# Other staging offsets for a second layer's token tiles, and a loop on three engines issued in source order

## The chip, the cores and the metric

The kernel runs on one core of a Trainium2 chip. TensorE does matmuls and transposes into PSUM (eight banks of 128 x 512 float32), ScalarE, VectorE and GpSimd do the elementwise work, SyncE issues most DMAs. The metric is the device time of one execution in microseconds, median over runs; lower is better.

## The reference

Two layers over 1024 latent tokens and 256 context tokens, width 1024, in float32:

```python
# layer 0: windowed attention, 16 query heads on 4 key heads, a sink logit per head
# layer 1: multi-head latent attention
hx = rms_norm(x, norm_g[i]) * (1.0 + scale_x[:, None]) + shift_x[:, None]
hc = rms_norm(ctx, norm_g[i]) * (1.0 + scale_c) + shift_c
# layer 1, inside project(h):
cq, ckv, kr, g = jnp.split(h @ w_in, [512, 512 + 256, 512 + 256 + 32], axis=-1)
q  = (rms_norm(cq, q_norm) @ w_uq).reshape(b, n, 16, 96)
kv = (rms_norm(ckv, kv_norm) @ w_ukv).reshape(b, n, 16, 128)
# softmax over all 1280 keys, then
yx = (ox * jax.nn.silu(gx)) @ w_out
x = x + gate_x[:, None] * yx
return rms_norm(x, final_g)
```

The change lies where layer 0 ends and layer 1 begins: the tokens that layer 0 has written are read again, normalized, scaled and shifted into `hx`/`hc`, and multiplied with the 288 columns of `w_in` that give the latent keys `ckv` and the rope keys `kr`.

## The kernel before

**Precision.** A float32 operand is kept as two reduced-precision parts, hi and lo. `split` makes them: ScalarE casts hi (L121), another engine subtracts it from the source for lo (L122; VectorE, or GpSimd where the caller says so). A product takes three matmuls (`mm3`, L126 to L128).

**Memory.** There is one hand-laid arena for hi/lo parts (`arena_r`) and one for float32 tiles (`arena_f`, 52 KB per partition). A `Ring` hands out fixed slots of an arena in turn. Stages of the kernel reuse the same bytes, so a tile that is laid over a tile of the stage before waits for the last reader there. Layer 0's attention probabilities are a ring of eight blocks of 2.5 KB, from 14 KB to 34 KB of `arena_f`: block i from 14 + 2.5 i. Each attention unit (a tile of 128 tokens and a key head) takes four blocks in turn; unit 38 takes blocks 0 to 3, the last one, unit 39, blocks 4 to 7. L611 transposes them and is their last reader.

**Layer 1's token tiles.** Ten tiles of 128 tokens go through these steps; two tiles make a pair `p`.
- `norm_x(i)`: load of 512 KB into a slot of ring `xr` (L210), square with sum on ScalarE (L212), a multiply-add on VectorE (L213), the power on GpSimd (L214), the scaling on VectorE (L215).
- `turn_x`: eight transposes on TensorE (L222) in two halves of four; each half takes the next bank of `pst` (6, 7, 6, 7 and so on) and ScalarE copies it (L223) into `xt`, a slot of ring `xtr`.
- `build_h(p)`: for each of eight 128-row blocks a scale-and-shift on VectorE (L236), and after every second one a cast for hi on ScalarE (L239) and a subtraction for lo on VectorE (L241), into `hT1[p]`.
- `kv_tile(ti)`: 24 matmuls of 288 columns from `hT1[p]` and the weights `wt1[0]` into a bank of `pss` (0 to 5); the square on ScalarE (L953), L954 on VectorE, the power on GpSimd (L955), the scaling on VectorE (L992), and the rope keys (L995, or L268 and L273). Its `rest` is put on a list: two transposes (L1005) into the next bank of `pst`, and their `split` (L121 and L122, both reading that bank) into `ckvT`.
- `flush(2)` runs the oldest `rest` while more than two are on the list, so `rest` of tile ti runs in iteration ti + 2.
- `g_tile(6, p)`: 48 matmuls of 256 columns and a silu (L1091), stored to DRAM (L1093).

`fetch1(k)` loads a weight block in pieces through the ring `stg` (L262) and splits each piece. Block 0 is that of `kv_tile`, block 6 that of `g_tile(6, .)`, blocks 1 and 2 those of `cq_tile`, which follows the loop. `wt1[0]`, `hT1[0]` and `hT1[1]` lie over `arena_r` tiles that layer 0's last attention units read; `wt1[6]`, `wt1[1]` and `hT1[2]` to `hT1[4]` lie over the output weights and operands of layer 0's last output projection (L669, L670), which is traced between `build_h(1)` and the loop.

**What orders the work.** The Tile framework tracks which bytes and which PSUM banks each instruction reads and writes and draws the waits. The order of an engine's instructions is chosen by a planner that walks a model of the engines and takes, of what is ready there, what stands first in the source. Inside a region `tc.manual_schedule(engines=...)` the named engines issue the region's instructions in source order; where those of outside fall between them stays with the planner. The second attention, later on, already stands in such a region. The loop around the change does not. Each engine executes its instructions in order: one that waits holds those behind it.

`pst` counts its calls: `turn_x` of tiles 0 to 5 takes 6 and 7 each, `rest` of tile 0 takes 6, `turn_x` of tile 6 takes 7 and then 6, `rest` 1 takes 7, tile 7 takes 6 and 7, `rest` 2 takes 6, tile 8 takes 7 and then 6, `rest` 3 takes 7, tile 9 takes 6 and 7, `rest` 4 takes 6, `rest` 5 takes 7.

Of the kernel before, what the change touches and what calls it, by code (L numbers as in the profile page):

```python
# [22 lines left out]
NT = TOK // 128  # L23
# [24 lines left out]
def shp(ap, *dims):  # L48
    n = 1
    for d in dims:  # L50
        n *= d
    ap = ap[:, 0:n]
    if len(dims) == 1:
        return ap
    names = "abcdefg"[: len(dims)]
    kw = {c: d for c, d in zip(names[1:], dims[1:])}
    return ap.rearrange("p (" + " ".join(names) + ") -> p " + " ".join(names), **kw)
# [3 lines left out]
def kernel(ctx: ExitStack, tc: tile.TileContext, t, out, dbg=None):  # L61
    nc = tc.nc
# [6 lines left out]
    F = cpool.tile([128, F_KB * KB], F32, name="arena_f")  # L69
# [16 lines left out]
    def r_at(kb, *dims):  # L86
        n = int(np.prod(dims))
        return shp(R[:, int(kb * KB) : int(kb * KB) + n], *dims)

    def f_at(kb, *dims):  # L90
        n = int(np.prod(dims))
        return shp(F[:, int(kb * KB) : int(kb * KB) + n], *dims)
# [26 lines left out]
    def split(hi, lo, src, lo_eng=None):  # L119

        nc.scalar.copy(hi, src)  # L121
        (lo_eng or nc.vector).tensor_sub(lo, src, hi.bitcast(F32))  # L122

    def mm3(o, a, b, first, last):
        (ah, al), (bh, bl) = a, b
        nc.tensor.matmul(o, ah, bh, start=first, stop=False)  # L126
        nc.tensor.matmul(o, al, bh, start=False, stop=False)  # L127
        nc.tensor.matmul(o, ah, bl, start=False, stop=last)  # L128
# [79 lines left out]
    def norm_x(src, xr, junk):  # L208
        x = xr.next()
        load(out=x, in_=src)  # L210
        st = sm_ring()
        nc.scalar.activation(junk, x, AF.Square, accum_out=st[:, 0:1])  # L212
        nc.vector.tensor_scalar(st[:, 1:2], st[:, 0:1], 1.0 / D, EPS, ALU.mult, ALU.add)  # L213
        nc.gpsimd.tensor_tensor(st[:, 2:3], st[:, 1:2], mhalf, ALU.pow)  # L214
        nc.vector.tensor_scalar_mul(x, x, st[:, 2:3])  # L215
        return x

    def turn_x(x, xt, j):
        for q in range(2):
            ps = shp(pst(), 4, 128)  # L220
            for c in range(4):
                nc.tensor.transpose(ps[:, c, :], x[:, (4 * q + c) * 128 : (4 * q + c + 1) * 128], ident)  # L222
            nc.scalar.copy(xt[:, 4 * q : 4 * q + 4, j * 128 : j * 128 + 128], ps)  # L223
# [33 lines left out]
    def load_w(dst, src, stage, nk, n, lo_eng=None, col0=0, k0=0):  # L257

        per = max(1, 512 // n)
        for k in range(k0, nk, per):  # L260
            st = shp(stage.next(), per, n)
            load(out=st, in_=src[k * 128 : (k + per) * 128, col0 : col0 + n].rearrange("(k p) n -> p k n", p=128))  # L262
            split(dst[:, 0, k : k + per, :], dst[:, 1, k : k + per, :], st, lo_eng or nc.gpsimd)

    def rope(o, u, cos, sin, nh, dim, tmp):

        hf = dim // 4
        nc.vector.tensor_mul(o, u, cos.unsqueeze(1).to_broadcast([128, nh, dim]))  # L268
        uv = u.rearrange("p h (a b c) -> p h a b c", a=2, b=2)
        sv = sin.rearrange("p (a b c) -> p a b c", a=2, b=2)  # L270
        tv = tmp.rearrange("p h (a b c) -> p h a b c", a=2, b=2)
        for b in range(2):
            nc.vector.tensor_mul(  # L273
                tv[:, :, :, b, :],
                uv[:, :, :, 1 - b, :],
                sv[:, :, b, :].unsqueeze(1).to_broadcast([128, nh, 2, hf]),
            )
        nc.gpsimd.tensor_add(o, o, tmp)
# [9 lines left out]
    stg = Ring(F, [4, 6, 8], 512)  # L288
    xr = Ring(F, [34, 38, 42, 48], 1024)
    ev = Ring(F, [38, 40, 42, 44], 512)  # L290
    junk = f_at(30, 512).bitcast(BF16)
# [3 lines left out]
    qst = Ring(F, [34, 48], 1024)  # L295
# [10 lines left out]
    class Pieces:  # L306
# [6 lines left out]
        def load(self, n=1):  # L313
            for _ in range(n):
                if self.todo:
                    bi, k = self.todo.pop(0)
                    c0 = blocks[bi]
                    st = shp(stg.next(), 2, 256)
                    src = w_in[k * 128 : (k + 2) * 128, c0 : c0 + 256]
                    load(out=st, in_=src.rearrange("(k p) n -> p k n", p=128))  # L320
                    self.held.append((bi, k, st))
# [370 lines left out]
    E = mybir.EngineType  # L692
# [233 lines left out]
    qn = f_at(8, 512)  # L926
    kvn = f_at(10, 256)
    junk = f_at(34.5, 512).bitcast(BF16)
    stg = Ring(F, [30, 32.25, 49.5], 576)
    xr = Ring(F, [22, 26, 45], 1024)  # L930
    xtr = Ring(F, [14, 37], 2048)
    ev = Ring(F, [2, 4, 6, 12], 512)
    ukK = r_at(134, 2, 2, 1024)
    ukV = r_at(64, 2, 2, 1024)
# [1 line left out]
    def src1(i):  # L936
        return x1_d[i * 128 : i * 128 + 128, :]
# [8 lines left out]
    def fetch1(bi, eng=None):  # L946
        kind, c0, n = blocks1[bi]
        nk = 4 if kind[0] == "q" else 8
        wt1[bi] = r_at(wst1[bi], 2, nk, n)
        load_w(wt1[bi], t["b_w_uq"] if kind[0] == "q" else w_in1, stg, nk, n, lo_eng=eng, col0=c0)  # L950

    def rstd(ps, n, st):
        nc.scalar.activation(junk[:, 0:n], ps, AF.Square, accum_out=st[:, 0:1])  # L953
        nc.vector.tensor_scalar(st[:, 1:2], st[:, 0:1], 1.0 / n, EPS, ALU.mult, ALU.add)  # L954
        nc.gpsimd.tensor_tensor(st[:, 2:3], st[:, 1:2], mhalf, ALU.pow)  # L955
        return st[:, 2:3]
# [18 lines left out]
    def flush(n=0):  # L975
        while len(pend) > n:
            pend.pop(0)()

    def kv_tile(ti):
        p, j = ti // 2, ti % 2  # L980
        W = wt1[0]
        ps = pss()
        for k in range(8):
            mm3(
                ps[:, 0:288],
                [hT1[p][:, s, k, j * 128 : j * 128 + 128] for s in range(2)],
                [W[:, s, k, :] for s in range(2)],
                k == 0, k == 7,
            )
        r = rstd(ps[:, 0:256], 256, sm_ring())  # L990
        e = ev.next()
        nc.vector.scalar_tensor_tensor(e[:, 0:256], ps[:, 0:256], r, kvn, ALU.mult, ALU.mult)  # L992
        kr = krF[:, ti : ti + 1, :]
        if ti < 2:
            nc.vector.tensor_copy(kr, shp(ps[:, 256:288], 1, 32))  # L995
        else:
            rope(
                kr, shp(ps[:, 256:288], 1, 32), cosb[:, ti - 2, :], sinb[:, ti - 2, :], 1, 32,
                shp(e[:, 288:320], 1, 32),
            )  # L1000

        def rest():
            pt = pst()
            for c in range(2):
                nc.tensor.transpose(pt[:, c * 128 : c * 128 + 128], e[:, c * 128 : c * 128 + 128], ident)  # L1005
            ts = slice(ti * 128, ti * 128 + 128)
            split(ckvT[:, 0, :, ts], ckvT[:, 1, :, ts], shp(pt[:, 0:256], 2, 128))

        pend.append(rest)
# [64 lines left out]
    def g_tile(bi, p, half=None, bank=None):  # L1074
        c0 = blocks1[bi][1]
        W = wt1[bi]
        if half != 1:
            gps[bi] = pss() if bank is None else bank
        ps = gps[bi]
        for j in (0, 1) if half is None else (half,):  # L1080
            for k in range(8):
                mm3(
                    ps[:, j * 256 : j * 256 + 256],
                    [W[:, s, k, j * 128 : j * 128 + 128] for s in range(2)],
                    [hT1[p][:, s, k, :] for s in range(2)],
                    k == 0, k == 7,
                )
        if half == 0:
            return
        gg = ev.next()  # L1090
        nc.scalar.activation(gg, ps, AF.Silu)  # L1091
        ch = (c0 - 800) // 128
        load(out=g1_d[ch : ch + 2, :, (p - 1) * 256 : p * 256].rearrange("c p n -> p c n"), in_=shp(gg, 2, 256))  # L1093

    nx = norm_x(src1(4), xr, junk)
    for ti in range(NT):
        n = ti + 3
        if 4 <= n < NT:
            if n % 2 == 0:
                xt = shp(xtr.next(), 8, 256)  # L1100
            turn_x(nx, xt, n % 2)
            if n + 1 < NT:
                nx = norm_x(src1(n + 1), xr, junk)
            if n % 2:
                build_h(n // 2, xt, hT1[n // 2], ada1.A, ada1.B, fast=True)
        kv_tile(ti)
        flush(2)
        if ti > 1 and ti % 2:
            g_tile(6, ti // 2)
    fetch1(2, nc.vector)  # L1110
    for ti in range(8):
        cq_tile(ti)
        flush(2)
    fetch1(3, nc.vector)
    fetch1(4)
    rtmp = Ring(F, [14, 28], 512)
    qst = Ring(F, [16, 20, 24, 37, 41, 45], 1024)
    for ti in range(8):
        qr_tile(ti)
        flush(2)  # L1120
# [368 lines left out]
    E = mybir.EngineType  # L1489
# [174 lines left out]
```

## Time and profile before

| | |
|---|---|
| median of 3 runs | 1632.33 us (1632.14 to 1632.37) |
| the profiled execution | 1635.02 us, of which the profile's span is 1633.2 us |
| TensorE busy over the span | 1587.7 us (97%) |
| VectorE, ScalarE, GpSimd busy | 927.3, 805.0 and 702.5 us |
| mean granted TensorE clock | 0.993 |

The profile is of one execution. Its times count from the start of the span. Of a matmul the engine's start is recorded and its end modelled, so matmuls overlap in the listing; the distance from one start to the next is its pace. A merged row gives the start of the first instruction, the time from there to the end of the last, and their number. A bracket at the end of a row is the engine's idle time just before it and what ended that. Layer 0's attention ends near 724 us, the loop of the change runs from there to about 814 us.

### The profile page before, as it was taken

The page shows a single profiled execution, that of the slowest core. Times are in us where ns is not written, and L with a number is a line of the kernel's source. Part 1 is how long each engine was busy: PE and PEld are TensorE (multiplying, and loading weights), DVE is VectorE, ACT ScalarE, POOL GpSimd, SP SyncE. Part 2 cuts the span into 40 slices and gives each one's busy share as a digit, 9 for nine tenths or more (in the row PEclk, how much of TensorE's full clock was granted, in tenths as well). Part 3 has the DMA queues.
Part 4 walks back from the last instruction along what each step waited for, and adds up shares of the span by engine and source line. Part 5 has one row for each costly group of instructions (what it writes and reads, how often), then busy time and mean ns, then how long its engine had stood idle before and what let it go on. Part 6 is the DMA issues. An engine that isn't in the chain of part 4 may idle for free.

```text
span 1633.2 us, 27119 instructions
## 1 busy us (share of the span) xinstructions
PE 1587.7 (97%) x9938; PEld 1240.4 (76%) x9938; DVE 927.3 (57%) x1993; ACT 805.0 (49%) x1558; POOL 702.5 (43%) x684
## 2 busy tenths in 40 slices
PE   7999999999999999998999999999999999999998
PEld 4787787887878888877998899566766766766587
DVE  3515550538888888868425203566566566566354
ACT  3432232359777777777313323454555554544321
POOL 1241121115453333334105230478687688688510
PEclk9999999999999999999999999999999999999999
DMA  7447774444343333335105743213233223244151
GB/s 247 162 149 214 223 213 144 128 152 107 94 121 94 91 91 91 91 119 188 45 2 167 264 144 91 65 37 94 66 94 83 80 74 94 65 126 116 54 174 65
DMA packets 147205, 192.70 MB, mean 118 GB/s; under 512 B 13936, under 2 KB 84208, under 8 KB 147072
## 3 DMA queue, kind: packets, MB, share of 16 engines
q1 hardware_dynamic: 145456, 188.94, 38.5%
q10 hardware_dynamic: 1616, 2.04, 0.4%
q8 instruction: 78, 1.28, 0.3%
q14 instruction: 55, 0.45, 0.1%
HBM read 144.77 MB, written 46.15 MB: 117 GB/s over the span
## 4 chain that ended last, share of the span: by engine, by line
PE 85%; ACT 5%; DVE 4%; issue 2%; DMA 2%; POOL 1%; ACTq 0%; POOLq 0%; SPq 0%; DVEq 0%
PE PB L126 15%; PE PB L127 14%; PE PB L128 14%; PE PB L1291 11%; PE PB L1313 8%; PE PB L1260 5%; PE PB L621 4%; PE PB L611 3%; PE PB L583 2%; PE PB L584 2%; PE PB L181 2%; ACT arena_f L593 1%; PE PB L1263 1%; ACT arena_r L121 1%; ACT arena_f L632 1%
## 5 line engine op out<-in xcount | busy, mean ns | idle before, releaser
L126 PE MATMUL PB<-arena_r 128*128 128x512 f32 (+3 forms) x1496 | 509.9, 342 | 4.5 <-ACT arena_r L387 1.6
L127 PE MATMUL PB<-arena_r 128*128 128x512 f32 (+3 forms) x1496 | 503.3, 337 | 3.1 <-DVE arena_r L388 1.4
L128 PE MATMUL PB<-arena_r 128*128 128x512 f32 (+3 forms) x1496 | 501.2, 335 | 0.2 <-DVE arena_r L122 0.2
L1305 POOL TENSOR_TENSOR arena_f<-arena_f 128x512 f32<-128x512 f32 x252 | 328.9, 1305 | 110.5 <-ACT arena_f L1297 94.3
L126 PEld LDWEIGHTS PB<-arena_r 128*128 128x128 f32 x1496 | 284.2, 191 | 50.2 <-issue 15.0
L127 PEld LDWEIGHTS PB<-arena_r 128*128 128x128 f32 x1496 | 285.2, 191 | 31.6 <-DVE arena_r L388 3.1
L128 PEld LDWEIGHTS PB<-arena_r 128*128 128x128 f32 x1496 | 285.1, 191 | 28.4 <-DVE arena_r L122 0.4
L1265 DVE TENSOR_REDUCE arena_f<-PB 128x1 f32<-128x1280 f32 x128 | 190.2, 1486 | 118.5 <-PE PB L1263 109.7
L122 POOL TENSOR_TENSOR arena_r<-arena_f,arena_r 128x512 fp32r<-128x512 f32 x88 | 115.5, 1327 | 308.5 <-ACT arena_r L121 250.9
L1291 PE MATMUL PB<-arena_r 64*128 64x512 f32 (+1 forms) x1600 | 230.8, 393 | 2.9 <-ACT arena_f L1297 1.5
L1297 ACT ACTIVATE arena_f<-PB 128x1024 f32<-128x1024 f32 x160 | 164.2, 1027 | 125.5 <-PE PB L1291 85.3
L1291 PEld LDWEIGHTS PB<-arena_r 64*128 64x128 f32 (+1 forms) x1600 | 175.2, 185 | 28.5 <-ACT arena_f L1297 3.3
L590 DVE CUSTOM_DVE_ANT_0 arena_f<-PB,arena_f,small 128x256 f32<-128x256 f32 (+1 forms) x288 | 145.1, 522 | 25.1 <-PE PB L584 18.6
L1313 PE MATMUL PB<-arena_f 128*64 128x512 f32 x640 | 144.4, 597 | 0.0
L122 DVE TENSOR_TENSOR arena_r<-PB,arena_r 128x512 fp32r<-128x512 f32 (+1 forms) x186 | 123.1, 670 | 22.7 <-ACT arena_r L121 22.0
L593 ACT ACTIVATE arena_f<-arena_f,small 128x640 f32<-128x640 f32 (+2 forms) x160 | 119.3, 746 | 28.4 <-DVE small L592 27.5
L621 PE MATMUL PB<-arena_r 128*128 128x512 f32 x336 | 123.6, 440 | 3.5 <-ACT arena_f L632 3.3
L121 ACT CAST arena_r<-arena_f 128x512 fp32r<-128x512 f32 (+2 forms) x137 | 82.2, 609 | 81.1 <-DVE arena_f L485 11.5
L121 ACT CAST arena_r<-PB 128x512 fp32r<-128x512 f32 (+1 forms) x186 | 104.0, 570 | 31.6 <-PE PB L611 30.9
L611 PE MATMUL PB<-ident,arena_f 128*128 128x128 f32 x672 | 111.5, 274 | 1.4 <-ACT arena_f L593 0.9
L1313 PEld LDWEIGHTS PB<-arena_f 128*64 128x64 f32 x640 | 43.1, 136 | 81.3 <-issue 80.5
L611 PEld LDWEIGHTS PB<-ident,arena_f 128*128 128x128 f32 x672 | 83.5, 140 | 20.5 <-ACT arena_f L593 5.1
(180 smaller groups left out, 2002.4 us busy)
## 6 DMA issues: line engine op xcount, KB each, us to landing
arena_f<-ada_w SPq DMA_DIRECT2D x47, 512.0 KB, 5.4
arena_r<-q_d SPq DMA_DIRECT2D x80, 256.0 KB, 4.1
arena_r<-qn_d SPq DMA_DIRECT2D x64, 256.0 KB, 3.7
arena_r<-qr_d SPq DMA_DIRECT2D x192, 64.0 KB, 3.2
arena_f<-a_w_in SPq DMA_DIRECT2D x40, 256.0 KB, 3.4
arena_f<-x SPq DMA_DIRECT2D x16, 512.0 KB, 5.1
g_d<-arena_f SPq DMA_DIRECT2D x32, 256.0 KB, 2.1
q_d<-arena_f SPq DMA_DIRECT2D x64, 128.0 KB, 2.4
```

The lines of the kernel that those rows point to most:

```text
L121: nc.scalar.copy(hi, src)
L122: (lo_eng or nc.vector).tensor_sub(lo, src, hi.bitcast(F32))
L126: nc.tensor.matmul(o, ah, bh, start=first, stop=False)
L127: nc.tensor.matmul(o, al, bh, start=False, stop=False)
L128: nc.tensor.matmul(o, ah, bl, start=False, stop=last)
L611: nc.tensor.transpose(pt[:, h, :], self.Ps[h][:, ci * 128 : ci * 128 + 128], ident)
L621: nc.tensor.matmul(self.pv, V[:, self.chunks[ci], self.g, :], PT[:, s], start=ci == 0 and s == 0, stop=ci == self.m - 1 and s == 1,)
L1265: nc.vector.reduce_max(self.mx[:, 32 + b : 33 + b], flat, AX.X, negate=True)
L1291: nc.tensor.matmul(S[:, t], k[r, c : c + 128], q[r], start=j == 0, stop=j == 4)
L1297: nc.scalar.activation(E, self.S, AF.Exp)
L1305: eng.tensor_add(self.acc, self.acc, E[:, t])
L1313: nc.tensor.matmul(self.pv[p : p + 64], Vq[:, cs[t], self.h % 4, :], E[:, t], start=i == 0, stop=i == 4)
```

## The change

It does three things.
1. The offsets of `stg`, `xr` and `xtr` in `arena_f` are others, and with them those of `rtmp` and `qst` further on, with the same number and size of slots. In KB: `xr` goes from 22, 26, 45 to 48, 14, 18; `xtr` from 14, 37 to 24.25, 38.75; `stg` from 30, 32.25, 49.5 to 36.5, 22, 32.25. 48 to 52 held a gate of layer 0 that only its context tiles use; 38 to 48 hold small tiles of the last attention units.
2. The loop over the ten tiles stands in a region in which TensorE, ScalarE and VectorE issue in source order.
3. In the source `build_h` stands behind `kv_tile` and ahead of `flush`, where it stood ahead of `kv_tile`; and `fetch1(2)`, which followed the loop, stands in its last iteration ahead of the last `g_tile`.

```diff
-    stg = Ring(F, [30, 32.25, 49.5], 576)
-    xr = Ring(F, [22, 26, 45], 1024)
-    xtr = Ring(F, [14, 37], 2048)
+    stg = Ring(F, [36.5, 22, 32.25], 576)
+    xr = Ring(F, [48, 14, 18], 1024)
+    xtr = Ring(F, [24.25, 38.75], 2048)
...
     nx = norm_x(src1(4), xr, junk)
-    for ti in range(NT):
-        n = ti + 3
-        if 4 <= n < NT:
-            if n % 2 == 0:
-                xt = shp(xtr.next(), 8, 256)
-            turn_x(nx, xt, n % 2)
-            if n + 1 < NT:
-                nx = norm_x(src1(n + 1), xr, junk)
-            if n % 2:
+    with tc.manual_schedule(engines={E.PE, E.Activation, E.DVE}):
+        for ti in range(NT):
+            n = ti + 3
+            if 4 <= n < NT:
+                if n % 2 == 0:
+                    xt = shp(xtr.next(), 8, 256)
+                turn_x(nx, xt, n % 2)
+                if n + 1 < NT:
+                    nx = norm_x(src1(n + 1), xr, junk)
+            kv_tile(ti)
+            if 4 <= n < NT and n % 2:
                 build_h(n // 2, xt, hT1[n // 2], ada1.A, ada1.B, fast=True)
-        kv_tile(ti)
-        flush(2)
-        if ti > 1 and ti % 2:
-            g_tile(6, ti // 2)
-    fetch1(2, nc.vector)
+            flush(2)
+            if ti == NT - 1:
+                fetch1(2, nc.vector)
+            if ti > 1 and ti % 2:
+                g_tile(6, ti // 2)
...
-    rtmp = Ring(F, [14, 28], 512)
-    qst = Ring(F, [16, 20, 24, 37, 41, 45], 1024)
+    rtmp = Ring(F, [14, 20], 512)
+    qst = Ring(F, [16, 24.25, 28.25, 39, 43, 47], 1024)
```

## The prediction

> **What bounds the kernel now.** I read the page's busy shares first, then the busy time in stretches around the change, then the timelines of TensorE, ScalarE and VectorE there, and last SyncE's waits.
>
> ```profile
> span 1633.2 us, 27119 instructions
> PE 1587.7 (97%) x9938; PEld 1240.4 (76%) x9938; DVE 927.3 (57%) x1993; ACT 805.0 (49%) x1558; POOL 702.5 (43%) x684
> PE 85%; ACT 5%; DVE 4%; issue 2%; DMA 2%; POOL 1%; ACTq 0%; POOLq 0%; SPq 0%; DVEq 0%
> ...
> 710.00:724.00 14.00, 13.08 (x70) 10.19 (x69) 8.49 (x25) 7.63 (x19) 7.21 (x10) 1.00 0.17 58
> 724.00:739.00 15.00, 13.89 (x70) 10.87 (x69) 10.21 (x28) 12.23 (x27) 3.08 (x4) 1.00 0.89 296
> 739.00:755.00 16.00, 12.38 (x92) 11.42 (x91) 15.15 (x27) 10.84 (x23) 8.57 (x7) 1.00 0.64 203
> 755.00:774.00 19.00, 15.77 (x106) 15.22 (x105) 14.69 (x37) 14.10 (x30) 9.85 (x14) 0.82 0.52 156
> 774.00:800.00 26.00, 26.00 (x211) 26.00 (x210) 15.79 (x50) 12.04 (x29) 3.99 (x9) 1.00 0.06 21
> ```
>
> TensorE sets the time: it is busy 97% and is 85% of the chain that ended last. (In the stretches the columns are length, then busy time of TensorE, its weight loads, VectorE, ScalarE and GpSimd, the granted clock, the DMA share.) So the change is worth what it does to TensorE's holes. From 724 to 774 us, the end of layer 0 and the first part of the loop, it idles 1.11 + 3.62 + 3.23 = 7.96 us, and in the last of these stretches it ran at a clock of 0.82, which costs 15.77 x 0.18 = 2.84 us. From 774 us on it is never idle. **All that can be won is 7.96 + 2.84 = 10.8 us.**
>
> **Part one: the offsets.** Why are there holes?
>
> ```profile
> SPq L210 <- PE PB L611: 18.0, 1, 18.0
> ...
> 720.88 0.33 SPq L210 DMA_DIRECT2D arena_f<-x_d  x1
> ```
>
> The first token tile's load waits 18.0 us for the last attention's transposes, as its slot lies over probability blocks 3 and 4. DMAs are at a share of 0.17 before 724 and 0.89 behind it: all loads come at once, and the tiles' building follows 8 to 10 us late, with VectorE busy 15.15 of 16 us. With the new offsets the first tile (48 KB) waits for nothing of the attention, the second and third (blocks 0 to 3) for unit 38 instead of unit 39; the copies of the turned tiles (24.25 to 32.25, blocks 4 to 7) still wait for unit 39, and the casts into `hT1` and `wt1[0]` for its last product. So three loads, three squares and three scalings move ahead of 724 us. They have room there: VectorE idles 5.5 and ScalarE 6.4 of the 14 us before 724. In exchange some 10 us of building are no longer late, and VectorE's work for pairs 0 and 1 should be ahead of the 11 us or so of matmuls of the last output projection. I take it that everything up to the third `kv_tile` runs without a hole; bounds for this part: nothing won up to there, and all won.
>
> **Part two: source order in the loop, where it bites.** Two engines now do what the planner avoided. The rows are of iterations 3 and 4 before:
>
> ```profile
> 766.46 0.37 ACT L121 CAST arena_r<-PB 128x256 fp32r<-128x256 f32 x1
> ...
> 760.29 5.61 DVE L236 TENSOR_SCALAR arena_f<-arena_f,small 128x256 f32<-128x256 f32 x8
> 765.83 2.49 DVE L241 TENSOR_TENSOR arena_r<-arena_f,arena_r 128x512 fp32r<-128x512 f32 x4
> 768.89 0.41 DVE L122 TENSOR_TENSOR arena_r<-PB,arena_r 128x256 fp32r<-128x256 f32 x1
> ...
> 767.37 0.44 PE L1005 MATMUL PB<-ident,arena_f 128*128 128x128 f32 x2 [2.86 <-ACT arena_f L223]
> 769.46 1.05 PE L222 MATMUL PB<-ident,arena_f 128*128 128x128 f32 x4
> ```
>
> The four transposes at 769.46 are the second half of tile 6. They write bank 6, where `rest` 0 has its transposes, so they cannot start before the lo part of `rest` 0 (L122 at 768.89) has read it, and that stood behind the eight L236 and four L241 of `build_h(2)`. The planner put 30-odd matmuls of `g_tile` in between, and the wait shown is 2.86 us. In the next round it even moved the lo part of `rest` 2 into the middle of `build_h(3)`:
>
> ```profile
> 774.40 1.71 DVE L236 TENSOR_SCALAR arena_f<-arena_f,small 128x256 f32<-128x256 f32 x5 [1.18 <-ACT arena_f L223]
> 776.02 1.29 DVE L241 TENSOR_TENSOR arena_r<-arena_f,arena_r 128x512 fp32r<-128x512 f32 x2
> 777.22 1.05 DVE L236 TENSOR_SCALAR arena_f<-arena_f,small 128x256 f32<-128x256 f32 x3
> 778.19 0.15 DVE L954 TENSOR_SCALAR small<-small 128x1 f32<-128x1 f32 x1
> 778.25 0.41 DVE L122 TENSOR_TENSOR arena_r<-PB,arena_r 128x256 fp32r<-128x256 f32 x1
> ...
> 780.19 1.29 DVE L241 TENSOR_TENSOR arena_r<-arena_f,arena_r 128x512 fp32r<-128x512 f32 x2 [0.61 <-ACT arena_r L239]
> ...
> 775.22 1.21 ACT L239 CAST arena_r<-arena_f 128x512 fp32r<-128x512 f32 x2 [0.37 <-DVE arena_f L236]
> 779.55 1.13 ACT L239 CAST arena_r<-arena_f 128x512 fp32r<-128x512 f32 x2
> ```
>
> After the change TensorE's order is `kv_tile(2)`, `rest` 0 (bank 6), tile 6's halves (banks 7 and 6), `kv_tile(3)`, `rest` 1, `g_tile`; VectorE's is the tail of `kv_tile(2)`, all of `build_h(2)`, the lo part of `rest` 0. So tile 6's second half waits for the whole of `build_h(2)`, and `kv_tile(3)` and everything behind it wait with it. The same meets tile 8 with `rest` 2 behind `build_h(3)`. `build_h(4)` holds nobody: tile 9 is turned already, and `kv_tile(8)` comes behind `kv_tile(7)` and a `g_tile`.
>
> The hole, counted from TensorE's last issue of `kv_tile(2)`:
>
> ```profile
> 794.91 0.38 PE L1005 MATMUL PB<-ident,arena_f 128*128 128x128 f32 x2
> 795.17 0.38 ACT L953 ACTIVATE arena_f<-PB 128x256 bf16<-128x256 f32 x1 [1.56 <-PE PB L128]
> ...
> 796.49 0.48 DVE L992 SCALAR_TENSOR_TENSOR arena_f<-PB,small,arena_f 128x256 f32<-128x256 f32 x1 [0.66 <-POOL small L955]
> 797.15 0.41 DVE L122 TENSOR_TENSOR arena_r<-PB,arena_r 128x256 fp32r<-128x256 f32 x1
> ...
> 777.16 0.38 PE L1005 MATMUL PB<-ident,arena_f 128*128 128x128 f32 x2
> 777.38 0.60 PE L222 MATMUL PB<-ident,arena_f 128*128 128x128 f32 x4
> 777.74 0.38 PE L126 MATMUL PB<-arena_r 128*128 128x288 f32 x1
> ```
>
> - VectorE is through the tile's tail (square, L954, GpSimd's power, L992, rope) at 797.15 - 794.91 = 2.24 us.
> - One of four steps of `build_h`, in order: two L236 to the cast's start 775.22 - 774.40 = 0.82; cast to L241 780.19 - 779.55 = 0.64 (VectorE now stands waiting, as the next L236 is behind that L241); L241's pace (777.22 - 776.02) / 2 = 0.60. Together 2.06, four times 8.24 us.
> - The lo part 0.41. Sum 10.9 us.
> - Meanwhile TensorE has `rest` 0 (0.22) and tile 6's first half (0.36). **Hole: 10.9 - 0.58 = 10.3 us, twice: 20.6 us.**
>
> Bounds of a hole: the same twelve VectorE instructions with no waiting take 8 x 0.33 + 4 x 0.60 = 5.0, hole 7.1; with GpSimd in the way (L236 at 5.61 for eight, beside its splits) about 3 more, 13.3. GpSimd's eight splits of blocks 6 and 1 wait for the last output projection in both kernels, so the last few can fall into the first hole: I add 1.0 us, between 0 and 3.
>
> The clock: after the 2.86 us hole it fell.
>
> ```profile
> 765.00:770.00 5.00, 2.63 (x18) 2.63 (x19) 4.75 (x15) 4.88 (x11) 0.81 (x3) 0.88 0.22 62
> 770.00:775.00 5.00, 5.00 (x35) 5.00 (x34) 2.92 (x9) 3.62 (x7) 1.57 (x3) 0.77 0.38 121
> ```
>
> That dip cost 2.63 x 0.12 + 5.00 x 0.23 = 1.47 us. I take it once for each hole, 2.9 us; bounds 0 and twice that, for a longer hole may cost more. [...]
>
> A small third wait: tile 5's turning needs tile 5 normalized, which ScalarE can only start behind tile 4's copies.
>
> ```profile
> 773.09 1.04 PE L222 MATMUL PB<-ident,arena_f 128*128 128x128 f32 x8
> 773.88 0.38 PE L126 MATMUL PB<-arena_r 128*128 128x288 f32 x1
> ...
> 773.78 1.07 ACT L223 COPY arena_f<-PB 128x512 f32<-128x512 f32 x2
> 754.59 1.06 ACT L212 ACTIVATE arena_f<-arena_f 128x1024 bf16<-128x1024 f32 x1
> ...
> 757.65 1.54 PE L222 MATMUL PB<-ident,arena_f 128*128 128x128 f32 x8 [0.37 <-DVE small L954]
> ```
>
> Copies end 774.85 - 773.88 = 0.97 us behind the transposes, square to turning takes 757.65 - 754.59 = 3.06, and the `kv_tile` in between covers 777.16 - 773.88 = 3.28: 0.75 us open. For tiles 6 and 8 the same wait lies inside the holes, for 7 and 9 a `g_tile` covers it.
>
> **Edits at nothing.** `fetch1(2)` in the region: its casts wait for `kv_tile(9)` to leave `wt1[0]` in both kernels, and the last `g_tile` (48 matmuls) and the first half of `cq_tile(0)` lie over them; uncovered it would be one DMA wait of about 4 us. The moves of `rtmp` and `qst` keep number and size, at a place where TensorE is never idle. SyncE gets the three earlier loads ahead of the last probability-stage loads; with DMAs at 0.17 they hold up nothing.
>
> **The sum.** -10.8 + 0.75 + 20.6 + 2.9 + 1.0 = +14.5 us. The profiled execution took 1635.02 us, its span 1633.2 and 1.8 around it; with 14.5 it would show a span of 1647.7 and 1649.5 in all. It stands 2.69 above the median of the runs, so the median goes from 1632.33 to **1646.8 us**.
>
> **The rivals.**
> - *Not slower: the holes are not there.* At tile 6's second half, if TensorE finds other work or bank 6 is read in time; decided where a hole falls under (10.05 - 2.9) / 2 = 3.6 us. Then 1632.33 - 10.05 = 1622.3. For it: the matmuls of `cq_tile` stand outside the region and could be put in. Against: their banks come after those of later `kv_tile`s in the rotation of six, and the rows 768.89 and 769.46 show the bank's wait as it is.
> - *One hole only*, or two at the low bound: 1632.33 - 10.05 + 14.2 + 2.9 = 1639.4 with both at 7.1; with one at 10.3 and its dip, 1634.0.
> - *The early start doesn't come*: the turned tiles' slots still lie over blocks 4 to 7, and SyncE's loads may be queued behind waiting ones, so the offsets don't set the tiles apart as they say. Of the 10.8, 2.86 and its dip of 1.47 lie behind `kv_tile(2)` and go anyway; 6.5 stay: 1653.3. For it: VectorE at 15.15 of 16 us. Against: three of its scalings leave that stretch.
> - *Bigger holes* (13.3 each, twice the dip for one): 1632.33 - 10.05 + 26.6 + 4.4 = 1653.3.
>
> **How the numbers follow.** The forecast 0.62 (1641 to 1650); no holes 0.08; small or single hole 0.10; no early start 0.08; bigger holes 0.12. A measurement of this kernel tells 0.2% (3.3 us) from no change. Faster 0.08, same 0.05 (the half of the single-hole case), slower 0.87. The range 1637 to 1654 leaves out the no-hole case, the single hole and the far ends.
>
> **What would show it.** Right: TensorE idle for some 10 us between the halves of tiles 6 and 8 (L222), released by VectorE's L122, a clock below 1 behind each; VectorE with waits on L239 ahead of each L241; little idle between 724 us and the third `kv_tile`; the first L210 well ahead of 720.88 us. Wrong: no such holes, or `build_h` on VectorE in under 6 us.

## The result and the profile after

The changed kernel takes 1663.49 us (median of 4 runs, 1659.32 to 1665.49) against 1632.35 us for the kernel before on the same chip: a ratio of 1.0175, with a 95% interval of 1.0163 to 1.0188, some 31 us slower. The forecast had the direction right, but its range ended at 1654: less than half of the loss was foreseen.

The first page of the profile after, and its busy time in the stretches of the prediction (length, then TensorE, weight loads, VectorE, ScalarE, GpSimd, granted clock, DMA share):

```profile
span 1660.4 us, 27113 instructions
PE 1590.6 (96%) x9938; PEld 1244.1 (75%) x9938; DVE 927.9 (56%) x1993; ACT 804.6 (48%) x1558; POOL 700.0 (42%) x684
...
710.00:724.00 14.00, 11.87 (x62) 8.72 (x60) 8.21 (x26) 9.69 (x23) 8.27 (x12) 1.00 0.31 105
724.00:739.00 15.00, 12.64 (x65) 9.64 (x65) 11.11 (x28) 10.94 (x26) 2.08 (x2) 1.00 0.65 212
739.00:755.00 16.00, 8.17 (x38) 7.26 (x39) 15.88 (x23) 8.55 (x16) 10.10 (x8) 0.75 0.71 214
755.00:774.00 19.00, 11.66 (x81) 10.99 (x79) 7.88 (x24) 8.08 (x18) 5.47 (x8) 0.86 0.38 122
774.00:800.00 26.00, 16.80 (x116) 16.36 (x116) 9.24 (x28) 9.77 (x20) 2.80 (x6) 0.83 0.10 31
800.00:830.00 30.00, 26.68 (x196) 26.68 (x197) 10.81 (x31) 9.24 (x23) 2.18 (x5) 0.86 0.03 9
```

The span grew by 27.2 us. TensorE's idle time from 710 to 830 us, stretch length less busy time, is 2.13 + 2.36 + 7.83 + 7.34 + 9.20 + 3.32 = 32.18 us. Before it was 0.92 (14.00 - 13.08) and the 7.96 us of the prediction, 8.88 us, with none behind 774: 23.3 us more. The other engines do the same work; GpSimd and VectorE are no busier.

The holes behind that, from TensorE's timeline after:

```profile
724.78 0.50 PE L621 MATMUL PB<-arena_r 128*128 128x512 f32 x1 [2.23 <-DVE arena_r L122]
...
739.46 1.06 PE L222 MATMUL PB<-ident,arena_f 128*128 128x128 f32 x8 [1.63 <-DVE arena_f L215]
...
751.31 0.61 PE L126 MATMUL PB<-arena_r 128*128 128x288 f32 x1 [7.37 <-DVE arena_f L669]
...
761.82 1.06 PE L222 MATMUL PB<-ident,arena_f 128*128 128x128 f32 x8 [0.27 <-DVE arena_f L215]
...
776.73 1.12 PE L222 MATMUL PB<-ident,arena_f 128*128 128x128 f32 x4 [9.74 <-DVE arena_r L122]
...
803.32 1.11 PE L222 MATMUL PB<-ident,arena_f 128*128 128x128 f32 x4 [9.69 <-DVE arena_r L122]
```

The last two are the forecast ones, ahead of the second halves of tiles 6 and 8. The first three were not forecast: one in the tail of layer 0's attention (724.78), one ahead of tile 3's turning (739.46), and one of 7.37 us ahead of `kv_tile(0)` (751.31). The row at 761.82 is tile 5's turning, the small third wait of the prediction. Here is how two of the three unforecast ones arise.

**Ahead of `kv_tile(0)`.** VectorE and GpSimd after, then TensorE and VectorE before:

```profile
745.96 1.35 DVE L236 TENSOR_SCALAR arena_f<-arena_f,small 128x256 f32<-128x256 f32 x1
...
747.94 1.04 DVE L670 TENSOR_TENSOR arena_f<-arena_f 128x512 f32<-128x512 f32 x1
748.91 1.75 DVE L241 TENSOR_TENSOR arena_r<-arena_f,arena_r 128x512 fp32r<-128x512 f32 x1
750.58 0.68 DVE L669 TENSOR_TENSOR arena_f<-PB,arena_f 128x512 f32<-128x512 f32 x1
...
745.27 4.84 POOL L122 TENSOR_TENSOR arena_r<-arena_f,arena_r 128x512 fp32r<-128x512 f32 x3 [4.22 <-ACT arena_r L121]
```

```profile
738.58 0.29 PE L126 MATMUL PB<-arena_r 128*128 128x288 f32 x1
...
745.08 0.40 PE L126 MATMUL PB<-arena_r 128*128 128x288 f32 x1
...
744.33 0.69 DVE L669 TENSOR_TENSOR arena_f<-PB,arena_f 128x512 f32<-128x512 f32 x1
```

`pss` has been called 54 times when `kv_tile(0)` comes; 54 is a multiple of six, so its accumulator is bank 0. The last output projection put its second half into that same bank (`PB[:, 0]`), and L669 reads it. L669 stands in VectorE's queue behind the building of pair 1, in which VectorE never rests from 739 to 754 us. Three instructions of that queue run beside GpSimd's splits and are slow: L236 takes 1.35 us there and 0.36 without GpSimd (two in 0.72, at 768.17 below), L241 1.75 and 0.69 (at 769.57 below), L670 1.04 and 0.68 (at 752.77). That is 2.4 of the 7.37 us; the rest is the order of VectorE's queue. Before, the planner ran `kv_tile(1)` at 738.58, in another bank, and `kv_tile(0)` from 745.08, behind the L669 at 744.33. In source order `kv_tile(0)` comes first, and everything behind it waits with it.

**The attention's tail.** VectorE and GpSimd after, and TensorE before at the same place:

```profile
723.38 0.75 DVE L215 TENSOR_SCALAR arena_f<-arena_f,small 128x1024 f32<-128x1024 f32 x1 [2.50 <-POOL small L214]
724.05 1.28 DVE L122 TENSOR_TENSOR arena_r<-PB,arena_r 128x512 fp32r<-128x512 f32 x2
...
719.32 0.73 POOL L644 TENSOR_TENSOR arena_f<-arena_f 128x256 f32<-128x256 f32 x1 [2.25 <-ACT arena_f L632]
...
722.79 0.55 POOL L214 TENSOR_TENSOR small<-small 128x1 f32<-128x1 f32 x1
```

```profile
719.28 0.73 PE L621 MATMUL PB<-arena_r 128*128 128x512 f32 x2 [0.43 <-ACT arena_f L632]
```

With its slot free early, tile 2's scaling (L215; those of tiles 0 and 1 start at 665.30 and 717.11) now stands in VectorE's queue ahead of the attention's last lo parts (L122 at 724.05). It waits 2.50 us for GpSimd's power (L214), which comes behind five operations of unit 38 (L644, from 719.32 on, to L649). TensorE waits for those lo parts: 2.23 us where the same place had cost 0.43.

**The forecast hole.** VectorE after, at tile 6:

```profile
768.17 0.72 DVE L236 TENSOR_SCALAR arena_f<-arena_f,small 128x256 f32<-128x256 f32 x2
769.57 0.69 DVE L241 TENSOR_TENSOR arena_r<-arena_f,arena_r 128x512 fp32r<-128x512 f32 x1 [0.68 <-ACT arena_r L239]
...
775.64 0.69 DVE L241 TENSOR_TENSOR arena_r<-arena_f,arena_r 128x512 fp32r<-128x512 f32 x1 [0.68 <-ACT arena_r L239]
776.25 0.42 DVE L122 TENSOR_TENSOR arena_r<-PB,arena_r 128x256 fp32r<-128x256 f32 x1
```

Four steps of (775.64 - 769.57) / 3 = 2.02 us, VectorE idle 0.68 us in each because the next L236 stands behind an L241 that waits for its cast; then the lo part of `rest` 0, and half a microsecond later the transposes.

**The clock.** Stretches of one microsecond behind the three long holes, those in which the clock came back:

```profile
757.00:758.00 1.00, 1.00 (x9) 0.98 (x9) 0.00 (x0) 0.47 (x3) 0.42 (x1) 0.80 0.72 168
...
781.00:782.00 1.00, 1.00 (x8) 1.00 (x8) 0.11 (x1) 0.00 (x0) 0.00 (x0) 0.85 0.00 0
...
808.00:809.00 1.00, 1.00 (x8) 1.00 (x7) 0.00 (x0) 0.00 (x0) 0.00 (x0) 0.70 0.00 0
```

TensorE starts again at half speed (0.50) and keeps it until about 757.4 (0.80 in that microsecond is 0.4 at half), 781.3 and 808.6: 6.1, 4.6 and 5.3 us behind the starts at 751.31, 776.73 and 803.32. Half of 16.0 us is 8.0 us of lost work, against the 2.84 us that the prediction counted before: 5.2 us more. With 23.3 us of idle time that makes 28.5, near the span's 27.2. (Read in this same way the kernel before loses 3.2 us, at half clock from 755.2 to 758.6 and from 768.9 to 772.3; then the sum is 28.1.) The medians lie 31.1 us apart because the profiled execution before stood 2.7 us above its median and the one after (1662.24 us) 1.25 us below.

### The profile page after: what moved, and what is told of

It is laid out like the page before. It is cut to its first block, busy times and chain, and to the rows that moved or that the text cites. A ratio compares the mean times of both kernels' runs of the same rounds, so it can differ in the third digit from the quotient of the medians.

```text
span 1660.4 us, 27113 instructions
## 1 busy us (share of the span) xinstructions
PE 1590.6 (96%) x9938; PEld 1244.1 (75%) x9938; DVE 927.9 (56%) x1993; ACT 804.6 (48%) x1558; POOL 700.0 (42%) x684
## 4 chain that ended last, share of the span: by engine, by line
PE 84%; DVE 6%; ACT 5%; issue 3%; POOL 1%; DMA 1%; POOLq 0%; SPq 0%; DVEq 0%; ACTq 0%
PE PB L126 15%; PE PB L127 14%; PE PB L128 14%; PE PB L1293 11%; PE PB L1315 8%; PE PB L1262 5%; PE PB L621 4%; PE PB L611 3%; PE PB L583 2%; PE PB L584 2%; PE PB L181 2%; ACT arena_f L593 1%; DVE arena_r L122 1%; PE PB L1265 1%; DVE arena_f L590 1%
## 5 line engine op out<-in xcount | busy, mean ns | idle before, releaser
L126 PE MATMUL PB<-arena_r 128*128 128x512 f32 (+3 forms) x1496 | 512.2, 344 | 10.7 <-DVE arena_f L669 7.4
L122 POOL TENSOR_TENSOR arena_r<-arena_f,arena_r 128x512 fp32r<-128x512 f32 x88 | 115.6, 1327 | 305.4 <-ACT arena_r L121 249.7
L122 DVE TENSOR_TENSOR arena_r<-PB,arena_r 128x512 fp32r<-128x512 f32 (+1 forms) x186 | 123.0, 670 | 18.7 <-ACT arena_r L121 18.1
```

## The experiments

All are timed against the kernel before on the same chip.

| kernel | what it is | median, us | ratio to before (95%) |
|---|---|---|---|
| after | | 1663.49 | 1.0175 (1.0163 to 1.0188) |
| e1_planner | after, without the region | 1635.10 | 1.0009 (1.0000 to 1.0019) |
| e2_region | after, with the old offsets | 1663.24 | 1.0182 (1.0167 to 1.0197) |
| e11_no_pe | after, TensorE not in the region | 1640.20 | 1.0032 (1.0021 to 1.0043) |
| e3_flush | after, `flush` ahead of `build_h` | 1654.84 | 1.0132 (1.0116 to 1.0147) |
| e5_later | after, `build_h` one iteration later | 1655.72 | 1.0125 (1.0110 to 1.0140) |
| e12_g_even | after, `g_tile` one iteration earlier | 1657.83 | 1.0141 (1.0123 to 1.0160) |
| e4_bank | after, another bank for the projection | 1661.29 | 1.0170 (1.0155 to 1.0186) |
| e6_one_early | after, only one early slot | 1661.35 | 1.0165 (1.0150 to 1.0180) |
| e7_all | four of these mends together | 1652.80 | 1.0110 (1.0094 to 1.0125) |
| e8_planner_one | e6 without the region | 1634.48 | 1.0004 (0.9993 to 1.0015) |
| e9_planner_f1 | e8, bank of e4, block 1 later | 1633.20 | 0.9988 (0.9979 to 0.9997) |
| e10_before_f1 | before, bank of e4, block 1 later | 1632.37 | 0.9981 (0.9972 to 0.9990) |

### Which part loses: the offsets or the order?

e1_planner keeps the new offsets and the new source order but leaves the order of the engines to the planner:

```diff
-    with tc.manual_schedule(engines={E.PE, E.Activation, E.DVE}):
+    if True:
```

> The changed kernel without the region: new offsets and new source order, but the planner orders all engines. Theory (the strict order makes the two holes of 9.7 us at tiles 6 and 8 and the 7.4 us hole ahead of the first kv_tile, which waits for a PSUM bank): all three go or shrink below 4 us, the hole of 2.2 us in the attention's tail stays because the early scaling of tile 1 stands there by the offsets: 1630 to 1640 us. Rival (the offsets make the loss, since the loads and scalings come at a bad time): above 1650 us.

e2_region keeps the region and goes back to the old offsets:

```diff
-    stg = Ring(F, [36.5, 22, 32.25], 576)
-    xr = Ring(F, [48, 14, 18], 1024)
-    xtr = Ring(F, [24.25, 38.75], 2048)
+    stg = Ring(F, [30, 32.25, 49.5], 576)
+    xr = Ring(F, [22, 26, 45], 1024)
+    xtr = Ring(F, [14, 37], 2048)
```

with `rtmp` and `qst` as they were too.

> The region and the new source order with the old offsets. Theory: the two holes of about 9.7 us are there as in the changed kernel, and kv_tile(0) waits for the VectorE read of bank 0 by the last output projection, where the planner ran kv_tile(1) first; no hole in the attention's tail. 1652 to 1662 us. Rival (the offsets make the loss): below 1642 us.

Without the region the loss is gone (1.0009, inside its expectation); with the region and the old offsets it is as large as before (1.0182). The offsets are worth nothing that can be measured. Both kernels keep the new source order; the region with the old one, `build_h` ahead of `kv_tile`, was not run. TensorE's four largest holes in e1_planner, and the one at tile 6 in e2_region:

```profile
727.30 0.79 PE L621 MATMUL PB<-arena_r 128*128 128x512 f32 x1 [2.23 <-DVE arena_r L122]
743.43 1.30 PE L222 MATMUL PB<-ident,arena_f 128*128 128x128 f32 x8 [2.02 <-DVE arena_f L215]
755.36 0.40 PE L126 MATMUL PB<-arena_r 128*128 128x288 f32 x1 [1.71 <-DVE arena_f L669]
764.16 1.06 PE L222 MATMUL PB<-ident,arena_f 128*128 128x128 f32 x8 [1.40 <-ACT arena_f L212]
```

```profile
776.66 1.12 PE L222 MATMUL PB<-ident,arena_f 128*128 128x128 f32 x4 [9.17 <-DVE arena_r L122]
```

From 710 to 830 us TensorE idles 9.01 us in e1_planner, about the 8.88 of the kernel before, at other places. The early start is real, and the time it wins is given back in the attention's tail and in later waits.

e2_region came 1.2 us above its range. Its holes at tiles 6 and 8 (9.17 and 9.68 us) were expected, and there is none in the attention's tail. But the expected hole ahead of `kv_tile(0)` is not there either: with the old offsets the tiles themselves are late, and TensorE idles 2.30, 1.81, 2.99 and 2.35 us ahead of turnings between 743 and 767 us. So the bank's hole of 7.37 us needs the region and the new offsets together.

### Which engine's order?

```diff
-    with tc.manual_schedule(engines={E.PE, E.Activation, E.DVE}):
+    with tc.manual_schedule(engines={E.Activation, E.DVE}):
```

> The changed kernel with ScalarE and VectorE in source order and TensorE's order left to the planner. Theory (the two 9.7 us holes are TensorE standing at bank 6 because VectorE's order holds the lo part of rest 0 and rest 2 behind a whole building; TensorE's own order only matters as far as there is other work to take): the planner puts g_tile's 48 matmuls or the next kv_tile ahead of the half that waits, so each 9.7 us hole shrinks to between 0 and 5 us, and the 7.4 us hole ahead of kv_tile(0) goes as kv_tile(1) can run first: 1636 to 1650 us. Rival (VectorE's and ScalarE's order alone makes the loss, since the work they release comes late whatever TensorE does meanwhile): 1655 us or more, with the same total of idle time at other places.

1640.20 us, ratio 1.0032: with TensorE free, some 23 of the 31 us come back. VectorE in that run, and TensorE's busy time in two stretches of 30 us:

```profile
770.77 0.69 DVE L241 TENSOR_TENSOR arena_r<-arena_f,arena_r 128x512 fp32r<-128x512 f32 x1 [0.69 <-ACT arena_r L239]
...
776.85 0.69 DVE L241 TENSOR_TENSOR arena_r<-arena_f,arena_r 128x512 fp32r<-128x512 f32 x1 [0.69 <-ACT arena_r L239]
777.46 0.42 DVE L122 TENSOR_TENSOR arena_r<-PB,arena_r 128x256 fp32r<-128x256 f32 x1
```

```profile
755.00:785.00 30.00, 27.26 (x209) 25.92 (x208) 14.96 (x39) 15.82 (x34) 9.34 (x13) 1.00 0.40 129
785.00:815.00 30.00, 28.69 (x217) 26.99 (x216) 15.57 (x45) 12.33 (x30) 3.65 (x8) 1.00 0.03 10
```

VectorE goes through the same lockstep, (776.85 - 770.77) / 3 = 2.03 us a step, and the lo part of `rest` 0 comes at 777.46, no earlier than in the kernel after. But TensorE idles 2.74 and 1.31 us in these stretches, which in the kernel after hold the two holes of 9.7 us, and the clock stays at 1.00: the planner puts a `g_tile` and a `kv_tile` where source order has nothing that may run. So a late lo part is harmless by itself. The loss is TensorE standing in order behind it.

### Mending the loop within source order

e3_flush takes the waiting `rest` out from behind the building:

```diff
             kv_tile(ti)
+            flush(2)
             if 4 <= n < NT and n % 2:
                 build_h(n // 2, xt, hT1[n // 2], ada1.A, ada1.B, fast=True)
-            flush(2)
```

> The changed kernel with flush ahead of build_h in the source, still in the region. Theory: the lo part of rest 0 and rest 2 stands ahead of the building on VectorE, so tile 6's and tile 8's second halves wait only for the kv_tile's tail: holes of about 2 us instead of 9.7, their clock dips smaller: 1663.5 - 15 - 2 to 4 = 1644 to 1648 us; the 7.4 us hole ahead of kv_tile(0) stays. Rival (the building itself is late for kv_tile(4), so the time only moves): above 1656 us.

e5_later puts a pair's building into the next iteration, behind the next tile's turning and normalizing and ahead of `kv_tile`:

```diff
+            if hq:
+                build_h(hq[0], hq[1], hT1[hq[0]], ada1.A, ada1.B, fast=True)
+                hq = None
+            if 4 <= n < NT and n % 2:
+                hq = (n // 2, xt)
             kv_tile(ti)
-            if 4 <= n < NT and n % 2:
-                build_h(n // 2, xt, hT1[n // 2], ada1.A, ada1.B, fast=True)
```

> The changed kernel, in the region, with build_h(p) traced one iteration later: behind the next tile's turning and scaling, ahead of that iteration's kv_tile. Theory: then neither the bank of rest 0 (lo part on VectorE) nor that of tile 6 (copies on ScalarE) is queued behind a building, so both holes of 9.7 us and their clock dips go, the 7.4 us ahead of kv_tile(0) and the 2.2 us in the attention's tail stay: 1663.5 - 19.4 - 2 to 5 = 1639 to 1642 us. Rival (the building is on the path whatever its place, as kv_tile(4) waits for it): above 1650 us.

e12_g_even gives TensorE work for the hole:

```diff
-            if ti > 1 and ti % 2:
+            if ti > 1 and ti % 2 == 0:
                 g_tile(6, ti // 2)
```

> The changed kernel, all three engines in source order, with g_tile(6, .) at the end of iterations 2, 4, 6 and 8 instead of 3, 5, 7 and 9: its 48 matmuls then stand in TensorE's queue between rest 0 (rest 2) and the halves of tile 6 (tile 8), as the planner had put them. Theory (the holes are TensorE with nothing in its queue that may run during the building): each 9.7 us hole loses 48 x 0.12 = 5.8 us and becomes 3.9 us, the time falls by 11.7 us and up to 3 us of clock, to 1648 to 1653 us. Rival (work that is moved into a hole is missing elsewhere: kv_tile(3) and kv_tile(5) have no g_tile behind them any more to cover the normalizing of tiles 7 and 9): holes of 2 us or more each ahead of the turning of tiles 7 and 9, and 1654 us or more.

e3_flush and e5_later missed their expectations: 1654.84 and 1655.72 us where 1644 to 1648 and 1639 to 1642 were expected; e5_later is in its rival's range, e3_flush between the two. e12_g_even came at 1657.83, on its rival's side. TensorE's holes in e3_flush, e5_later and e12_g_even, two of each:

```profile
770.95 0.66 PE L222 MATMUL PB<-ident,arena_f 128*128 128x128 f32 x4 [1.64 <-DVE arena_r L122]
...
778.81 0.64 PE L1005 MATMUL PB<-ident,arena_f 128*128 128x128 f32 x2 [4.00 <-ACT arena_f L223]
```

```profile
770.65 0.66 PE L222 MATMUL PB<-ident,arena_f 128*128 128x128 f32 x4 [1.65 <-DVE arena_r L122]
784.54 1.12 PE L222 MATMUL PB<-ident,arena_f 128*128 128x128 f32 x4 [3.64 <-DVE arena_r L122]
```

```profile
779.79 0.66 PE L222 MATMUL PB<-ident,arena_f 128*128 128x128 f32 x4 [4.24 <-DVE arena_r L122]
787.70 0.66 PE L222 MATMUL PB<-ident,arena_f 128*128 128x128 f32 x4 [1.90 <-DVE arena_r L122]
```

Each time the 9.7 us hole goes and another wait stands close behind. In e3_flush it is ScalarE: the copies of tile 6 (L223) are queued behind the casts of the building, and `rest` 1's transposes need their bank; 1.64 + 4.00 us are left of 9.74. In e5_later it is the next `rest`, behind the later building. In e12_g_even 4.24 us are left of the first hole (3.9 was expected), and a new one of 1.90 comes in tile 7, which no longer has a `g_tile` to cover it; what it waits for is the lo part of `rest` 1 (L122), not the normalizing that the rival named. The 2.2 and 5.7 to 7.4 us holes ahead of the loop stay in all three.

The clock takes part of the gain too. From 700 to 830 us, TensorE's idle time falls from 32.2 us to 24.0 in e3_flush, 20.6 in e5_later and 23.6 in e12_g_even. What it loses at half clock is 8.0 us in the kernel after, and 7.9, 10.7 and 12.7 in these three: shorter holes, but more of them with a dip behind.

### Ahead of the loop

e4_bank takes `kv_tile(0)`'s bank out of the projection's way:

```diff
-                ps[c] = PB[:, 0, :] if last and c else pso()
+                ps[c] = PB[:, 2, :] if last and c else pso()
```

> The changed kernel with the second half of the last output projection in bank 2 instead of bank 0. Theory: kv_tile(0), whose bank is 0, no longer waits for that half's read on VectorE (L669 at 750.58) and starts some 7 us sooner, but tile 4's turning, next on TensorE, then waits for its scaling (L215 at 751.2), so only 3 to 6 us come back: 1657 to 1661 us. Rival (kv_tile(0) waits for its operands, not for the bank): no change, 1662 to 1665 us.

e6_one_early leaves only the first token slot apart from the probabilities:

```diff
-    xr = Ring(F, [48, 14, 18], 1024)
-    xtr = Ring(F, [24.25, 38.75], 2048)
+    xr = Ring(F, [48, 24.25, 28.25], 1024)
+    xtr = Ring(F, [14, 38.75], 2048)
```

> The changed kernel with other offsets: xr at 48, 24.25, 28.25 and xtr at 14, 38.75, so that only tile 0 is loaded and scaled inside the attention's tail, and tiles 1 and 2 wait for unit 39 as before. Theory (the 2.2 us hole in the tail is VectorE waiting at tile 1's early scaling for GpSimd's power, behind which the attention's lo parts stand): the hole goes; tiles 1 to 3 come later, which the wait ahead of kv_tile(0) may take back: 1659 to 1664 us. Rival (the hole is the tail's own): it stays at 2.2 us.

e6_one_early came as expected, e4_bank 0.3 us above its range. TensorE in e4_bank and in e6_one_early:

```profile
755.69 1.94 PE L222 MATMUL PB<-ident,arena_f 128*128 128x128 f32 x8 [5.89 <-DVE arena_f L215]
```

```profile
720.31 0.73 PE L621 MATMUL PB<-arena_r 128*128 128x512 f32 x2 [0.43 <-ACT arena_f L632]
...
743.18 1.06 PE L222 MATMUL PB<-ident,arena_f 128*128 128x128 f32 x8 [2.98 <-DVE arena_f L215]
```

Without the shared bank the wait for L669 is gone, so the bank did hold `kv_tile(0)`. TensorE then stands 5.89 us at tile 4's turning, as VectorE reaches that scaling no earlier. Without the two early scalings the tail hole is back to 0.43 us, so they made it (by the rows above it is tile 2's scaling that waits, not tile 1's); tile 3's turning waits 2.98 instead.

### All mends together

e7_all is e5_later, e4_bank and e6_one_early in one, with the fetch of weight block 1 in the loop's seventh iteration instead of ahead of the output projection:

```diff
-    fetch1(1)
...
             flush(2)
+            if ti == 6:
+                fetch1(1)
```

> In the region: build_h one iteration later, the last output projection's second half in bank 2, only tile 0 early, and block 1 of the weights fetched in the loop's seventh iteration instead of ahead of the loop, so that half of GpSimd's splits leave the stretch. Theory (the loss is the sum of these waits): between 1626 and 1636 us, no hole over 3 us. Rival (source order costs by itself, through the short waits of every tile): above 1640 us.

1652.80 us, where 1626 to 1636 had been expected: it is in the rival's range. The best of the kernels with three engines in source order is still 1.1% slower than the kernel before. Two of its holes:

```profile
758.51 1.94 PE L222 MATMUL PB<-ident,arena_f 128*128 128x128 f32 x8 [3.36 <-DVE small L954]
...
781.91 1.12 PE L222 MATMUL PB<-ident,arena_f 128*128 128x128 f32 x4 [3.63 <-DVE arena_r L122]
```

No long one is left, but six of 1.9 to 3.6 us between 740 and 805, all ahead of a turning. Four end with the lo part of a `rest` (L122), two with VectorE's work on a tile's norm. From 700 to 830 us TensorE idles 20.2 us and loses 10.2 more at half clock: short holes cost the clock as well.

### The planner's order with these mends

e8_planner_one is e6_one_early without the region; e9_planner_f1 adds the bank of e4_bank and the later block 1 of e7_all; e10_before_f1 is the kernel before with the last two edits alone.

> As the run without the region (new source order, planner on all engines), with the offsets by which only tile 0 is early. Theory (the gain of the offsets is eaten by the 2.2 us hole in the tail and by VectorE's queue ahead of kv_tile): the tail's hole goes, the rest is about as before: 1631 to 1634 us. Rival: the offsets cost nothing in the tail, no difference from the run without the region, 1635 us.

> The changed kernel without the region (the order is the planner's), with the first token slot at 48 KB and the other two at 24.25 and 28.25, the turned tiles at 14 and 38.75, the last output projection's second half in bank 2, and weight block 1 fetched in the loop's seventh iteration instead of ahead of the output projection. Theory (GpSimd's splits of block 1 slow VectorE's building of pair 1, and the bank of kv_tile(0) waits for that; the planner hides what is left): the idle time from 700 to 830 us falls from the 12.9 us of the planner's run with these offsets to 4 to 7 us, and the time to 1626 to 1631 us. Rival (what comes earlier only makes the next thing late, as in all runs before): idle stays at 9 us or more and the time within 3.3 us of the kernel before, 1630 to 1637 us.

> The kernel before, with only two edits: the last output projection's second half in bank 2 instead of bank 0, and weight block 1 fetched in the loop's seventh iteration. Its idle time in this stretch is 8.9 us and its dip 2.8 us. Theory (these two are what the planner's order lacks, not the offsets): 1626 to 1631 us. Rival (the first token load behind the attention sets the start of the building, and the planner had already put other matmuls where the bank waited): within 3.3 us of the kernel before, 1630 to 1637 us.

e8_planner_one is level with the kernel before; at 1634.48 us it lies between its theory and its rival and decides nothing. The other two are 2 and 3 us faster, with medians in the rival's range (1630 to 1637) and not in the theory's (1626 to 1631). In e9_planner_f1 the idle time from 700 to 830 us is 9.2 us, on its rival's side (9 or more); its small gain is in the clock, with 1.4 us lost at half speed against 3.2 in the kernel before. In e10_before_f1 the idle time is 7.1 us against 8.9. For e10_before_f1 the interval (0.9972 to 0.9990) excludes 1, but the size is about what a measurement of this kernel can tell. Its building beside GpSimd's splits is as slow as before: only block 1's splits were moved, and those of block 6 remain in its place. That the splits cost VectorE its time is read from the durations above; no run took all of them away.

## Why the prediction was right or wrong

**Right: the two holes.** Forecast 10.3 us each at the halves of tiles 6 and 8, measured 9.74 and 9.69. A step of `build_h` was forecast at 2.06 and took 2.02; the wait on L239 ahead of each L241 is there; `build_h(4)` holds nobody. The wait at tile 5 was forecast at 0.75 us and is 0.27. The 1.0 us for GpSimd's splits in the first hole was not needed. These terms together came 2.7 us below the forecast.

**Wrong: "I take it that everything up to the third `kv_tile` runs without a hole", and the step under it, "three loads, three squares and three scalings move ahead of 724 us. They have room there".** The term was -7.96 us of idle time. What failed is the room, not the early start. Apart from the two holes and tile 5's wait, 32.18 - 9.74 - 9.69 - 0.27 = 12.48 us of idle time are left where the forecast left 0.92: 11.6 us off, the largest error. The three loads did come early, the first at 525.25 us, the next two and the fourth here:

```profile
711.73 0.33 SPq L210 DMA_DIRECT2D arena_f<-x_d  x1
...
712.59 0.43 SPq L210 DMA_DIRECT2D arena_f<-x_d  x1
...
730.55 0.42 SPq L210 DMA_DIRECT2D arena_f<-x_d  x1
```

The three scalings, at 665.30, 717.11 and 723.38, came ahead of 724 us as well. But room was counted as VectorE's idle time in the stretch, and not by the place in its queue: a scaling that waits for GpSimd holds the attention's lo parts behind it (2.23 us; e6_one_early shows it). The fourth tile, for which the prediction has no term, takes tile 0's slot again, which tile 0's transposes read until 729.3; its load at 730.55 was too late for tile 3's turning (1.63 us). And the part was costed as if the planner's order still held up to the third `kv_tile`, though the prediction itself says that the region puts the loop in order: nobody asked where `kv_tile(0)`'s bank came from, while the same question was asked of bank 6. That is the 7.37 us hole (e4_bank).

**Mis-sized: the clock.** The term was 2.9 us for two dips, so about nothing net of the dip of before. Measured are three dips with 8.0 us lost, 5.2 net. A dip was priced by the one behind a 2.86 us hole, at 1.47 us from the averages of two stretches; with half clock from 768.9 to 772.3 and TensorE busy throughout, that dip itself cost 1.7. Behind the three long holes of this kernel the clock started at half (0.50) and stayed there for 4.6 to 6.1 us. The upper bound, twice the price, came close for each of the two (2.3 and 2.65), and the third dip belongs to the hole that was missed.

By the three terms so far the forecast's +14.5 becomes 14.5 + 11.6 + 5.1 - 2.7 = 28.5 us, against 27.2 in the spans.

**Misread: the 2.86 us hole of the kernel before.** The prediction shows it as the wait for bank 6. The row behind that hole is `rest` 1's transposes (L1005 at 767.37), and what they wait for is bank 7, whose copy on ScalarE stands behind three casts of the building (L239, from 764.65 to 766.56):

```profile
766.73 0.59 ACT L223 COPY arena_f<-PB 128x512 f32<-128x512 f32 x1
```

It is the wait that was left in e3_flush (4.00 us), so the rows of the kernel before already held that second queue. That TensorE is never idle from 774 us on holds to about 900 us only; behind that it idles some 12.6 us, which the change left nearly as they were.

**The rivals.** That the early start doesn't come had 6.5 us of idle time stay; the runs show that it comes and is given back elsewhere: e1_planner has as much idle time as the kernel before. "No holes, if TensorE finds other work" describes what the planner does as soon as TensorE is left out of the region (e11_no_pe); the argument against it was right for the kernel as it was changed.

## What to carry to other kernels

When an engine is put into source order, go through its whole queue in the region and ask of each instruction which buffer or bank it waits for and what stands ahead of the last reader of that on the other engine, from the first instruction of the region on and not only where the loop looks tight. If the engine that bounds the kernel still has independent work, leave its order free: here the other two engines in source order cost about 5 us, and TensorE with them 31. A mend that breaks one long hole into several short ones can lose at the clock part of what it wins in idle time: e12_g_even has 8.6 us less idle time than the changed kernel and loses 4.7 us more at half clock. Idle time on an engine does not say that an early operation has room there; what counts is what it makes wait while it waits itself (here 2.23 us of TensorE's time ahead of 724.78, against 0.43 without the early scalings).

## What the runs showed of the hardware

In the changed kernel the granted clock behind idle times of 7.37, 9.74 and 9.69 us was 0.50 for 6.1, 4.6 and 5.3 us of continuous matmuls, and then 1.00; values between in longer stretches are mixes of these two, as the 0.80 from 757 to 758 us. With the part that lies inside the idle time, each of these stretches at half clock lasted 10.24 us: from 747.16 to 757.40, 771.05 to 781.29 and 798.36 to 808.60. The two of the kernel before between 700 and 830 us lasted 3.41 us each: 755.20 to 758.61 and 768.85 to 772.26.

The length of an idle time did not by itself decide whether the clock fell. In the kernel before it fell at 755.2, where the only idle times near are 1.12 and 0.55 us; in e11_no_pe no idle time between 740 and 755 us is longer than 2.31 us, and yet the clock fell behind that one: it was 0.65 from 743 to 744 us and 0.50 from 744 to 746.

```profile
742.78 1.45 PE L222 MATMUL PB<-ident,arena_f 128*128 128x128 f32 x8 [2.31 <-ACT arena_r L121]
```

The 2.23 us ahead of 724.78 in the changed kernel cost no clock: it was 1.00 from 710 to 745 us, and the next products of 512 columns started 0.23 us apart. In e1_planner, behind a hole of the same length ahead of 727.30, they started 0.42 us apart, and the clock from 724 to 755 us was 0.89. What made the difference was not shown.
